# Order of the products at the seams of a two-layer encoder step: first product behind the fifth, earlier operand split, one set of PSUM pools, first scores inside the last projection

## The chip, the cores and the metric

The kernel runs on one core of a Trainium2 chip. The metric is the device time of one execution in microseconds (us). A core has five engines that run their own instruction queues in order: TensorE (PE, matrix products into PSUM; PEld is its weight load), VectorE (DVE), ScalarE (ACT), GpSimd (POOL) and SyncE (SP, which issues DMAs). An instruction waits at the head of its queue until all that it needs is there, and everything behind it on that engine waits too.

## The reference, cut to what matters

576 tokens (512 of a new stream, 64 of a running one) of width 1024 go through two layers. Layer 0 mixes tokens by pooling, layer 1 by sparse attention; each is followed by an MLP of width 4096.

```python
def _mlp(h, w_up, w_down):
    u = jax.nn.relu(h @ w_up)
    return (u * u) @ w_down

# attention, per query block: 8 index heads choose the keys, 16 heads attend to them
score = einsum('bth,bths->bts', wi, relu(qi . kidx * 64**-0.5)); _, idx = top_k(score, n_sel)
p = softmax(q . k[idx] * 64**-0.5);  o = p @ v[idx];  x = x + o @ w_o
```

New keys, values and index keys are outputs too.

## The kernel before, in words

**Numbers.** Every float32 operand is split into a high and a low part, and a product is three matmuls (high by high, high by low, low by high). Weights arrive as `raw`, ACT casts them to the high part `wh` (L182), DVE subtracts to the low part `wl` (L183); for some blocks POOL does the latter. Activations are split in `split_x` (`xs`: ACT L295, DVE L296).

**MLP.** A layer's MLP is done as 2 by 2 blocks with seven products in place of eight (`seven`, L526 to L554): first product b11, then t1 and t2, then b21, t3, b22 and t4. Three PSUM banks a, b and c collect them. "Up" is the first half with relu and square, "Down" the second. A product is 12 matmuls of 128x288 (`product`, L496 to L506, all recorded at L505). After the fifth product, t3, DVE's instruction L613 reads bank b; the last product, t4, goes on in the same bank, so it waits for L613. The first product b11 of the Down that follows belongs to another bank.

**Attention.** Its input is split to `xs` (eight tiles) and multiplied by the projection weights (`pj`); after the first two projections `norm.stats` sums squares (`st`, ten matmuls), a short chain on ACT and DVE turns them into the row scales, and `norm.spread` brings them to all partitions (`rb`). Index scores (`ix`, L1188 to L1216) are formed, for the fourth block (i = 4) by POOL with a multiply (L1213) and an add (L1215) for each of eight heads, and `top_k` (L1224) on DVE masks all but the chosen keys in 16 or 18 rounds of two instructions. Then 40 units (block i, key head g, half s) run as a pipeline in `steps`: `scores` (`sc`, softmax on DVE and ACT, division by the sum on POOL), `transpose` (`pt`, copied to `pT` by ACT), `values` (`o`), and for the blocks i below TURNED = 2 also `normalise` (`on`, DVE L1365) and in `outputs` a transpose (`ot`). The output projection is done in part ahead (`wa`) between the units, the rest (`wo`) at the end.

**What sets the order.** The code's order gives priorities, and a scheduler with a cost model orders each engine's queue when the program is built; the pools decide which buffer a tile lies on, and a tile waits until the buffer's last reader is done. Before the change the PSUM pools are opened anew for the attention (two tiles of two banks, four of one) and again for its units (three and two), and the `xs` of attention lie partly on buffers that the last Down still reads.

Of the kernel before, what the change touches and what calls it, by code (L numbers as in the profile page):

```python
# [1 line left out]

# [1 line left out]

# [6 lines left out]
F32R = mybir.dt.float32r  # L11
# [24 lines left out]
FINAL_ASIDE = ((4, 5), (4, 5))  # L36
NORM_STEPS = (4, 11, 13)
PACE = (1, 2, 2)
PACED = 3 * NIDX - 1
SLOTS = {"xs": 8, "a": 3, "b": 3, "c": 4, "d": 3, "e": 2}  # L40
TURNED = 2
AHEAD = 3
HEADS = {"a": 512, "c": 1024, "d": 1024}
UNITS = 6
UNDER = 64
SPREAD_AT = 5
SPARE_UNITS = 6
RAWS = (4, 3)
# [9 lines left out]
def pool_dsa_kernel(ctx: ExitStack, tc: tile.TileContext, a, o):  # L58
# [59 lines left out]
    def const(shape, name, dt=F32, pool=None):  # L118
        return (pool or cst).tile(shape, dt, tag=name, bufs=1, name=name)
# [278 lines left out]
    def mlp(layer, gi, late=0, end=None):  # L398
# [101 lines left out]
        def product(bank, w, operand, factor, js, first=False):  # L500
            for j in js:
                wh, wl = (t[:, j * P:(j + 1) * P] for t in w)
                uh, ul = (operand(j, factor, part) for part in range(2))
                for i, (wt, ut) in enumerate(((wh, uh), (wh, ul), (wl, uh))):
                    pe.matmul(bank[:, :HT], wt, ut, start=first and j == 0 and i == 0, stop=j == 3 and i == 2,  # L505
                              skip_group_check=True)  # L506

        tasks = [0]

        def ahead(n=1):  # L510

# [7 lines left out]
        def take():  # L519
            if not ready:  # L520
                ahead()
            return ready.pop(0)

        def seven(operand, late, on):


            b, a_, c = (psum1(t) for t in "bac")
            on.banks = [t[:, :HT] for t in (a_, b, c)]
            w = take()
            product(b, w, operand, "b11", rows, True)  # L530
            tasks[0] += 1
            if tasks[0] <= SEEDED:
                pe.matmul(a_[:, :HT], w[0][:, :P], operand(0, "b11", 0), start=True, stop=True, skip_group_check=True)
            act.copy(a_[:, :HT], b[:, :HT])  # L534
            ahead()
            w1 = take()
            if late:
                w2 = take()
                product(c, w1, operand, "t1", rows[:3], True)
                product(b, w2, operand, "t2", rows[:3])  # L540
                product(c, w1, operand, "t1", rows[3:])
                on.c()
                ahead()
                product(b, w2, operand, "t2", rows[3:])
            else:
                product(c, w1, operand, "t1", rows, True)
                on.c()
                ahead()
                product(b, take(), operand, "t2", rows)
            on.b()  # L550
            ahead()
            for bank, factor, then in ((a_, "b21", on.lo0), (b, "t3", on.hi1), (c, "b22", on.hi0), (b, "t4", on.lo1)):
                product(bank, take(), operand, factor, rows)
                then()  # L554

        class Down:


            def __init__(self, q):
                self.lo, self.hi = ([x[2 * q + i][:, c0:c0 + HT] for i in range(2)] for c0 in (HT, 0))  # L560
# [481 lines left out]
            nc.sync.dma_start(o["pool"][s], tail[:, s])  # L1042


    def attention(parts):
        nonlocal x
        norm = Norm("a")
        twos = []
# [11 lines left out]
        for j in range(KT // 2):  # L1060
            nc.sync.dma_start(xd[:, 2 * j:2 * j + 2], x.t[j])
        cst = phase["cst2"]
        cs, sn = const([P, T], "cs", pool=phase["under"]), const([P, T], "sn", pool=cst)
        nc.sync.dma_start(cs, a["cos"])
        nc.sync.dma_start(sn, a["sin"])
        V = const([P, 9, 256], "V", pool=cst)
# [78 lines left out]

        pki = psum1("ki"), psum1("ki")
        project(pki, next_block(), xs)
        qi = const([P, NIDX, T - P], "qi", F32R, phase["under"])
        between = iter(())
        rope_qi(0, started)  # L1150
        pt = psum1("pj"), psum1("pj")
# [31 lines left out]
        nc.sync.dma_start(o["v_p"], V[:, 0:4])  # L1183
        nc.sync.dma_start(o["v_s"], V[:TS, 8])

        work = [None] + [const([P, (i + 1) * P if i < 4 else TP + TS], f"work{i}", pool=cst) for i in range(1, 5)]

        def index_scores(i):  # L1188
            np_ = P if i < 4 else TS
            wk = work[i]  # L1190
            n = wk.shape[1]
            q = qi[:, :, (i - 1) * P:(i - 1) * P + np_]
            on_pool = i == 4
            for h in range(NIDX):
                if i < 4:
                    pf = psum1("ix")
                    for part in range(2):
                        pe.matmul(pf[:, :n], q[:, h], kis[:, part, :n], start=part == 0, stop=part == 1)
                else:
                    pf = psum("ix")  # L1200
                    for part in range(2):
                        for c in range(2):
                            pe.matmul(pf[:TS, c, :HT], q[:, h], cki[:, part, c * HT:(c + 1) * HT], start=part == 0, stop=part == 1)
                if i < 4:
                    rl = pf
                    act.activation(rl[:, :n], pf[:, :n], AF.Relu, scale=0.125)
                else:
                    rl = tmp("rl")
                    act.activation(halves(rl[:TS]), pf[:TS, :, :HT], AF.Relu, scale=0.125)
                wcol = wi[:np_, i, h:h + 1]  # L1210
                if on_pool:
                    dst = rl[:np_, :n] if h else wk[:np_]
                    pool.tensor_tensor(dst, rl[:np_, :n], wcol.to_broadcast([np_, n]), ALU.mult)  # L1213
                    if h:
                        pool.tensor_tensor(wk[:np_], wk[:np_], dst, ALU.add)  # L1215
                elif h == 0:  # L1216
                    dve.tensor_scalar(wk[:np_], rl[:np_, :n], wcol, None, ALU.mult)
                else:
                    dve.scalar_tensor_tensor(wk[:np_], rl[:np_, :n], wcol, wk[:np_], ALU.mult, ALU.add)
                yield  # L1220
            if i < 4:
                dve.memset(wk[0:64, i * P + 64:(i + 1) * P], NEG)
# [10 lines left out]
                dve.tensor_scalar(wk[64:128], wk[0:64], -2e38, NEG, ALU.is_gt, ALU.mult)  # L1233
            dve.tensor_scalar(wk[:np_], wk[:np_], -2e38, NEG, ALU.is_gt, ALU.mult)

        mask0 = const([P, P], "mask0", pool=cst)
        pool.memset(mask0, 0.0)
        pool.memset(mask0[0:64, 64:128], NEG)
        work[0] = mask0
# [19 lines left out]
        class Unit:  # L1259
# [5 lines left out]
            def scores(self):  # L1265
# [2 lines left out]
                q = self.group.q  # L1268
                mask = work[i]
                pr = slot("c", "p", F32)  # L1270
                pt = psum("sc")
                if i < 4:
                    n = (i + 1) * P
                    nw = max(n, 256)
# [128 lines left out]
        def steps():  # L1403

            ranked = {0}
            for u in range(-AHEAD - 2, total + 2):
                if 0 <= u + AHEAD + 2 < total and units[u + AHEAD + 2].s == 0:
                    v = units[u + AHEAD + 2]
                    groups[v.i, v.g] = Group(v.i, v.g)
                if 0 <= u < total:  # L1410
                    units[u].transpose()
                if 0 <= u + AHEAD < total:
                    v = units[u + AHEAD]
                    if u + AHEAD >= 4:
                        next(index, None)
                    if v.i not in ranked:
                        ranked.add(v.i)
                        while done[0] < v.i * NIDX and next(index, 1) is None:
                            pass
                        top_k(v.i)  # L1420
                    v.scores()
                if 0 <= u - 1 < total:
                    units[u - 1].values()
                if 0 <= u - 2 < total and units[u - 2].s == 1:
                    units[u - 2].group.outputs()
                if u >= 18 and u % 2 == 0:
                    next(first_out, None)
                yield

        def pace():  # L1430

            due = 0
            for k in range(10 * KT):
                while due <= k and done[0] < PACED:
                    next(index)
                    due += PACE[min(done[0] // NIDX, 2)]
                    done[0] += 1
                yield

        done = [0]  # L1440
        index = (None for i in range(1, 5) for _ in index_scores(i))
        act.activation(small(8, "e1", 1), wi[:, 0], AF.Exp)
        between = pace()
        qd, ks = {}, []
        (k1, k2), st = rope(False)
# [6 lines left out]
            ks.append(t)  # L1452
        for g in range(NKV):
            qd[g] = rope_q(f"q{g}", g == NKV - 2, pool.tensor_copy if g == NKV - 1 else act.copy)
        parts.close()
        parts.enter_context(stage(ps=3, po=2))
        for _ in steps():
            pass
        act.activation(small(2, "rt2", 1), units[-1].group.sums, AF.Sqrt)
        for _ in first_out:  # L1460
# [5 lines left out]
        for m in range(KT):  # L1466
            pool.tensor_tensor(x[m][:, :2 * P], x[m][:, :2 * P], ahead[m], ALU.add)
        for m in range(KT):
            pt = psum("wo")
            project(pt, next_block(), ot, cols=((2 * P, T - 2 * P),))  # L1470
            dve.tensor_tensor(x[m][:, 2 * P:], x[m][:, 2 * P:], pt[:, 0, :T - 2 * P], ALU.add)

    x = Residual()
    with stage(more=RAWS[1]):
        with stage(xs=1, slots=1, tmps=6, ps=3, po=2):
            pool_mixer()
        with stage(xs=1, u=1, acts=1, xt=1, sums=4, ps=2, po=4):
            mlp(0, 1, late=KT)
    with stage(under=1, xs=1, slots=1, cst2=1, tmps=5), ExitStack() as parts:
        const([P, UNDER], "pad", pool=phase["under"])  # L1480
        parts.enter_context(stage(ps=2, po=4))
        attention(parts)
    with stage(u=1, xs=1, acts=1, xt=1, sums=4, more=RAWS[1], ps=2, po=4):
        mlp(1, 3, end=last)


# [94 lines left out]
```

## Time and profile before

| what | value |
|---|---|
| median of 3 runs | 1087.51 us (1086.35 to 1089.1) |
| the profiled execution | 1087.99 us |
| its span on the core | 1086.2 us |
| PE, DVE, ACT, POOL busy | 97%, 84%, 58%, 24% |

The profile gives, for one execution, when each instruction began and how long it took; in brackets behind a row stands how long its engine had been idle before it and which instruction ended that. Matmuls overlap: rows of 128x288 begin 0.13 us apart though each is shown with some 0.3 us. In a table by windows PEclk is the clock that TensorE was granted, as a share of its full 2.4 GHz; half of it is 1.2 GHz. The timeline puts the span in stages: pooling and the MLP of layer 0 to 418 us, attention's projections from there to 541 us, its units to 662 us, the output projection to 692 us, the MLP of layer 1 to the end.

### The profile page before, as it was taken

What the parts mean: (1) busy time and instruction counts of PE and PEld (TensorE: products, weight loads), DVE (VectorE), ACT (ScalarE), POOL (GpSimd) and SP (SyncE); (2) the same over time, 40 slices, a digit from 0 to 9 for tenths busy, and PEclk for the clock granted to TensorE, in tenths of its full rate; (3) what the DMA queues carried; (4) which work ended last, traced back from release to release, by engine and by line L of the source; (5) the groups of instructions that cost most, each with busy time, mean ns of one, the idle gap of its engine ahead of it and who ended that gap; (6) DMA issues with size and microseconds to landing.
All of it is one profiled execution on the core that took longest, in us unless ns stands there. A gap on an engine that the chain in (4) does not pass through costs nothing.

```text
span 1086.2 us, 21647 instructions
## 1 busy us (share of the span) xinstructions
PE 1050.9 (97%) x7942; PEld 1023.6 (94%) x7942; DVE 909.0 (84%) x1845; ACT 629.3 (58%) x1240; POOL 263.8 (24%) x285
## 2 busy tenths in 40 slices
PE   8999999999999999999989999999999999999996
PEld 8999998999999998999978888999999999999895
DVE  7888989879978977879998944688989879979974
ACT  8555466447546645454378786555467447547641
POOL 3100111111111100217687893000111111111001
PEclk9999999999999999999999999999999999999998
DMA  8333665666666664456642454433666666666512
GB/s 251 92 101 90 173 165 151 166 163 168 150 167 163 156 171 144 123 167 175 201 114 59 133 158 140 136 108 96 167 160 161 161 169 162 155 169 161 123 51 88
DMA packets 94459, 157.66 MB, mean 145 GB/s; under 512 B 13729, under 2 KB 25296, under 8 KB 94352
## 3 DMA queue, kind: packets, MB, share of 16 engines
q1 hardware_dynamic: 68720, 109.80, 31.9%
q0 software_dynamic: 15840, 28.84, 16.8%
q10 hardware_dynamic: 9792, 17.63, 5.1%
q8 instruction: 62, 1.02, 0.4%
q14 instruction: 45, 0.37, 0.1%
HBM read 141.15 MB, written 10.89 MB: 140 GB/s over the span
## 4 chain that ended last, share of the span: by engine, by line
PE 75%; DVE 12%; DMA 4%; ACT 3%; issue 3%; POOL 2%; SPq 0%; ACTq 0%; DVEq 0%; POOLq 0%
PE b L505 28%; PE c L505 14%; PE up L306 9%; PE a L505 7%; PE pj L306 3%; DVE wl L183 3%; PE wo L306 3%; DVE work L1231 2%; PE sc L1278 2%; DVE m L1230 2%; PE wa L306 1%; PE pt L1304 1%; PE pb L1012 1%; PE dn L306 1%; DVE u L477 1%
## 5 line engine op out<-in xcount | busy, mean ns | idle before, releaser
L182 ACT CAST wh<-raw 128x512 fp32r<-128x512 f32 (+1 forms) x316 | 195.1, 620 | 233.3 <-PE b L505 75.7
L183 DVE TENSOR_TENSOR wl<-raw,wh 128x512 fp32r<-128x512 f32 (+1 forms) x294 | 206.6, 705 | 35.6 <-ACT wh L182 28.1
L505 PE MATMUL b<-u,wh 128*128 128x288 f32 x992 | 203.2, 296 | 3.4 <-ACT a L534 1.6
L505 PEld LDWEIGHTS b<-u,wh 128*128 128x128 f32 x992 | 159.7, 188 | 5.5 <-ACT a L534 3.6
L182 ACT CAST wh<-sum 128x512 fp32r<-128x512 f32 x165 | 101.4, 620 | 82.9 <-PE b L505 37.5
L505 PE MATMUL b<-u,wl 128*128 128x288 f32 x496 | 145.7, 296 | 0.0
L183 DVE TENSOR_TENSOR wl<-sum,wh 128x512 fp32r<-128x512 f32 x165 | 112.0, 687 | 23.3 <-ACT wh L182 21.2
L239 POOL DMA_DIRECT2D sum<-in_w_down x31 | 27.1, 893 | 327.6 <-DMA sum<-in_w_down 128.7
L505 PE MATMUL c<-u,wh 128*128 128x288 f32 x496 | 103.3, 297 | 0.8 <-DVE u L477 0.5
L505 PEld LDWEIGHTS b<-u,wl 128*128 128x128 f32 x496 | 92.7, 188 | 0.0
L306 PE MATMUL up<-xs,wh 128*128 128x288 f32 x512 | 89.5, 296 | 0.2
L505 PE MATMUL b<-xt,wh 128*128 128x288 f32 x384 | 78.1, 297 | 8.0 <-DVE v L613 8.0
L477 DVE TENSOR_TENSOR u<-v,u 128x864 fp32r<-128x864 f32 (+2 forms) x100 | 82.0, 824 | 0.9 <-ACT u L474 0.5
L505 PEld LDWEIGHTS c<-u,wh 128*128 128x128 f32 x496 | 80.1, 188 | 2.3 <-DVE x L563 1.5
L474 ACT CAST u<-v 128x864 fp32r<-128x864 f32 (+2 forms) x100 | 72.7, 730 | 8.3 <-DVE v L492 5.6
L505 PE MATMUL b<-xs,wh 128*128 128x288 f32 x384 | 76.9, 295 | 0.0
L306 PEld LDWEIGHTS up<-xs,wh 128*128 128x128 f32 x512 | 74.6, 188 | 1.0 <-DVE v L463 0.6
L505 PE MATMUL c<-u,wl 128*128 128x288 f32 x248 | 73.3, 296 | 0.0
L239 POOL DMA_DIRECT2D sum<-in_w_up x24 | 20.8, 865 | 210.1 <-DVE wl L183 114.3
L505 PEld LDWEIGHTS b<-xt,wh 128*128 128x128 f32 x384 | 61.4, 188 | 9.6 <-DVE v L613 9.6
L306 PE MATMUL pj<-xs,wh 128*128 128x288 f32 x352 | 61.9, 295 | 1.3 <-ACT xs L295 1.2
L455 ACT ACTIVATE v<-v 128x288 f32<-128x288 f32 (+1 forms) x112 | 52.1, 476 | 17.2 <-DVE v L596 14.7
(287 smaller groups left out, 2731.3 us busy)
## 6 DMA issues: line engine op xcount, KB each, us to landing
raw<-in_w_up SPq DMA_DIRECT2D x128, 256.0 KB, 3.0
raw<-in_w_down SPq DMA_DIRECT2D x128, 256.0 KB, 2.8
raw<-in_w_o ACTq DMA_DIRECT2D x32, 256.0 KB, 3.0
sum<-in_w_down SPq DMA_DIRECT2D x31, 256.0 KB, 2.6
sum<-in_w_down POOLq DMA_DIRECT2D x31, 256.0 KB, 4.4
raw<-in_w_down POOLq DMA_DIRECT2D x31, 256.0 KB, 5.0
raw<-in_w_in ACTq DMA_DIRECT2D x30, 256.0 KB, 3.3
sum<-in_w_up SPq DMA_DIRECT2D x24, 256.0 KB, 2.8
```

The lines of the kernel that those rows point to most:

```text
L182: act.copy(h, src)
L183: how["sub"].tensor_tensor(l, src, f32(h), ALU.subtract)
L239: pool.dma_start(s1, odd[:, 512:], accum_op=ALU.add)
L306: pe.matmul(pt[h][:, :m] if isinstance(pt, tuple) else pt[:, h, :m], wt, xs[k][:, part, c:c + m], start=(k == 0 and i == 0), stop=(k == n ...
L455: act.activation(v, v, AF.Square)
L474: act.copy(u[:, f, 0], v[:, f])
L477: dve.tensor_tensor(u[:, f, 1], v[:, f], f32(u[:, f, 0]), ALU.subtract)
L505: pe.matmul(bank[:, :HT], wt, ut, start=first and j == 0 and i == 0, stop=j == 3 and i == 2, skip_group_check=True)
L1012: pe.matmul(pt[:, c0:c0 + rhs.shape[1]], lhs, rhs, start=n == 0, stop=n == len(steps) - 1)
L1230: dve.max(m8[:np_], wk[:np_])
L1231: dve.match_replace(wk[:np_], m8[:np_], wk[:np_], TAKEN)
L1278: pe.matmul(pt[:, hh, :nw], q[:, 2 * s + hh], ks[g][:, part, :nw], start=part == 0, stop=part == 1)
```

## The change

Six edits go together.

- In `seven`, when a Down follows the final Up, its first product is issued behind t3's last matmul (`tc.issue_after`).
- One set of PSUM pools (two tiles of two banks, four of one) serves from the MLP of layer 0 to that of layer 1. The scores of units with i below 2 and the output projection take one-bank tiles.
- The SBUF pools are laid out so that the attention's `xs` lie where the MLP's own `xs` lay; `qi` has a pool of its own behind them, `cs`, `sn`, one work tile and a mask take the place of the weight buffers.
- Five steps of the unit pipeline run inside the last projection (FIRST_STEPS), and all 24 index heads of blocks 1 to 3 are paced inside the projections.
- For block i = 4, the multiply by `wi` goes from POOL to ACT.
- For i below 2, `outputs` comes one unit later.

```diff
-PACED = 3 * NIDX - 1
+PACED = 3 * NIDX
+FIRST_STEPS = (66, 68, 70, 73, 76)
...
-            product(b, w, operand, "b11", rows, True)
+            with tc.issue_after(behind.pop()) if late and behind else nullcontext():
+                product(b, w, operand, "b11", rows, True)
...
-                product(bank, take(), operand, factor, rows)
+                ins = product(bank, take(), operand, factor, rows)
+                if factor == "t3" and on.final:
+                    behind.append(ins.ins)
...
-        cs, sn = const([P, T], "cs", pool=phase["under"]), const([P, T], "sn", pool=cst)
+        cs, sn = (const([P, T], s, pool=phase["under"]) for s in ("cs", "sn"))
...
-        qi = const([P, NIDX, T - P], "qi", F32R, phase["under"])
+        qi = const([P, NIDX, T - P], "qi", F32R, phase["queries"])
...
-                    pool.tensor_tensor(dst, rl[:np_, :n], wcol.to_broadcast([np_, n]), ALU.mult)
+                    act.activation(dst, rl[:np_, :n], AF.Copy, scale=wcol)
...
-                pt = psum("sc")
+                if i < TURNED:
+                    pt = halves(psum1("sc"))
+                else:
+                    pt = psum("sc")
...
-                if 0 <= u - 2 < total and units[u - 2].s == 1:
-                    units[u - 2].group.outputs()
+                for v in units[max(u - 3, 0):max(u - 1, 0)]:
+                    if v.s == 1 and v is units[u - 3 if v.i < TURNED else u - 2]:
+                        v.group.outputs()
...
+                if k in FIRST_STEPS:
+                    next(unit_steps)
                 yield
...
-        parts.close()
-        parts.enter_context(stage(ps=3, po=2))
-        for _ in steps():
+        for _ in unit_steps:
...
-            pt = psum("wo")
-            project(pt, next_block(), ot, cols=((2 * P, T - 2 * P),))
-            dve.tensor_tensor(x[m][:, 2 * P:], x[m][:, 2 * P:], pt[:, 0, :T - 2 * P], ALU.add)
+            pt = psum1("wo")[:, :T - 2 * P]
+            project(pt.rearrange("p (o t) -> p o t", o=1), next_block(), ot, cols=((2 * P, T - 2 * P),))
+            dve.tensor_tensor(x[m][:, 2 * P:], x[m][:, 2 * P:], pt, ALU.add)
...
-    with stage(under=1, xs=1, slots=1, cst2=1, tmps=5), ExitStack() as parts:
-        const([P, UNDER], "pad", pool=phase["under"])
-        parts.enter_context(stage(ps=2, po=4))
-        attention(parts)
-    with stage(u=1, xs=1, acts=1, xt=1, sums=4, more=RAWS[1], ps=2, po=4):
+    with stage(under=1, xs=1, queries=1, slots=1, cst2=1, tmps=5):
+        attention()
+    with stage(u=1, xs=1, acts=1, xt=1, sums=4, more=RAWS[1]):
```

What it moves, at three places of PE's queue. Line numbers after the change are 7 to 13 higher. The first is the end of the layer-0 MLP, before: `b_5231<-u` is the last Down's t3 and then, with `wh_5281`, its t4; `pj` are the first matmuls of the attention's projections on the split input `xs`.

```order
L505 MATMUL b_5231<-u_4673,wh_5247 128x288 x2
L505 MATMUL b_5231<-u_4673,wl_5248 128x288
L505 MATMUL b_5231<-u_4208,wh_5281 128x288 x2
L505 MATMUL b_5231<-u_4208,wl_5282 128x288
L505 MATMUL b_5231<-u_4363,wh_5281 128x288 x2
L505 MATMUL b_5231<-u_4363,wl_5282 128x288
L505 MATMUL b_5231<-u_4518,wh_5281 128x288 x2
L505 MATMUL b_5231<-u_4518,wl_5282 128x288
L505 MATMUL b_5231<-u_4673,wh_5281 128x288 x2
L505 MATMUL b_5231<-u_4673,wl_5282 128x288
L306 MATMUL pj_5446<-xs_5392,wh_5298 128x288 x2
L306 MATMUL pj_5523<-xs_5392,wh_5336 128x288 x2
```

The same place after the change, from the last rows of t3 to the first of the projections:

```order
L505 MATMUL b_5231<-u_4673,wh_5247 128x288 x2
L505 MATMUL b_5231<-u_4673,wl_5248 128x288
L306 MATMUL pj_5440<-xs_5386,wh_5298 128x288 x4
L306 MATMUL pj_5517<-xs_5386,wh_5336 128x288 x4
L306 MATMUL pj_5440<-xs_5386,wl_5299 128x288 x2
L306 MATMUL pj_5440<-xs_5386,wh_5298 128x288 x4
L306 MATMUL pj_5440<-xs_5386,wl_5299 128x288 x2
L306 MATMUL pj_5440<-xs_5395,wh_5298 128x288 x4
L306 MATMUL pj_5440<-xs_5395,wl_5299 128x288 x2
L306 MATMUL pj_5440<-xs_5395,wh_5298 128x288 x4
L306 MATMUL pj_5440<-xs_5395,wl_5299 128x288 x2
L306 MATMUL pj_5440<-xs_5406,wh_5317 128x288 x4
```

Forty projection matmuls in all now stand between t3 and t4 (six more follow the rows shown), where none stood.

A little later on PE stand the sums of squares `st` and the spreading of the scales `rb`, before:

```order
L356 MATMUL st_5503<-ones,s_875_5391 64x96
L306 MATMUL pj_5523<-xs_5401,wh_5336 128x288
L306 MATMUL pj_5523<-xs_5401,wl_5337 128x288 x2
L306 MATMUL pj_5523<-xs_5412,wh_5355 128x288 x4
L306 MATMUL pj_5523<-xs_5412,wl_5356 128x288 x2
L306 MATMUL pj_5523<-xs_5412,wh_5355 128x288 x4
L306 MATMUL pj_5523<-xs_5412,wl_5356 128x288 x2
L306 MATMUL pj_5523<-xs_5423,wh_5355 128x288 x4
L306 MATMUL pj_5523<-xs_5423,wl_5356 128x288 x2
L306 MATMUL pj_5523<-xs_5423,wh_5355 128x288 x4
L306 MATMUL pj_5523<-xs_5423,wl_5356 128x288 x2
L336 MATMUL rb_5588<-sq_5584,ones 128x288
```

And after the change:

```order
L356 MATMUL st_5497<-ones,s_874_5385 64x96
L306 MATMUL pj_5517<-xs_5417,wh_5355 128x288 x4
L306 MATMUL pj_5517<-xs_5417,wl_5356 128x288 x2
L306 MATMUL pj_5517<-xs_5417,wh_5355 128x288 x4
L306 MATMUL pj_5517<-xs_5417,wl_5356 128x288 x2
L336 MATMUL rb_5582<-sq_5578,ones 128x288
```

Between `st` and `rb` stood 27 matmuls, and 12 stand there now; 84 of the 96 that come before `rb` are ahead of `st`.

The third place is the start of the units, before: `pj_6820` is the last projection, `sc` are scores, `pt` transposes.

```order
L306 MATMUL pj_6820<-xs_5423,wh_6680 128x288 x4
L306 MATMUL pj_6820<-xs_5423,wl_6681 128x288 x2
L1278 MATMUL sc_6923<-k_6240,q_6917 128x256 x4
L1278 MATMUL sc_6935<-k_6240,q_6917 128x256 x4
L1278 MATMUL sc_6999<-k_6240,q_6920 128x256 x4
L1304 MATMUL pt_7010<-ident,p_6922 128x128 x2
L1278 MATMUL sc_7016<-k_6240,q_6920 128x256 x4
```

After the change, from the third of the scores on:

```order
L1288 MATMUL sc_6939<-k_6234,q_6811 128x256 x4
L306 MATMUL pj_6837<-xs_5406,wh_6679 128x288 x4
L306 MATMUL pj_6837<-xs_5406,wl_6680 128x288 x2
L306 MATMUL pj_6837<-xs_5406,wh_6679 128x288 x4
L306 MATMUL pj_6837<-xs_5406,wl_6680 128x288 x2
L306 MATMUL pj_6837<-xs_5417,wh_6679 128x288 x4
L306 MATMUL pj_6837<-xs_5417,wl_6680 128x288 x2
L306 MATMUL pj_6837<-xs_5417,wh_6679 128x288 x4
L306 MATMUL pj_6837<-xs_5417,wl_6680 128x288 x2
L1314 MATMUL pt_7001<-ident,p_6813 128x128 x2
L1288 MATMUL sc_7007<-k_6234,q_6811 128x256 x4
L1288 MATMUL sc_7036<-k_6239,q_6887 128x256 x4
```

The scores of the first three units lie among the projections, and the first transpose follows the last projection at once.

## Rows read from the trace of the kernel before

**Rows 1.** The page, busy time of each engine over the span.
```profile
PE 1050.9 (97%) x7942; PEld 1023.6 (94%) x7942; DVE 909.0 (84%) x1845; ACT 629.3 (58%) x1240; POOL 263.8 (24%) x285
```
**Rows 2.** PE's waits over the span: us in total, times, longest.
```profile
PE b L505 <- DVE v L613: 8.0, 7, 1.3
```
**Rows 3.** Busy us by window: PE, PEld, DVE, ACT, POOL, PEclk, DMA share, GB/s.
```profile
540.00:560.00 20.00, 16.89 (x123) 15.64 (x122) 18.47 (x72) 15.14 (x52) 18.02 (x16) 0.91 0.46 131
560.00:580.00 20.00, 16.92 (x127) 16.09 (x128) 16.45 (x62) 14.10 (x47) 14.80 (x12) 0.91 0.36 96
580.00:600.00 20.00, 19.68 (x172) 17.33 (x171) 19.30 (x58) 16.86 (x45) 16.15 (x25) 1.00 0.28 79
```
**Rows 4.** Timeline of PE, t3, b11 and t4: start, us, instruction, idle before.
```profile
184.89 0.29 PE L505 MATMUL b<-xs,wl 128*128 128x288 f32 x1
185.02 0.29 PE L505 MATMUL b<-u,wl 128*128 128x288 f32 x1
...
186.17 0.40 PE L505 MATMUL b<-u,wh 128*128 128x288 f32 x1
187.47 0.53 PE L505 MATMUL b<-xt,wh 128*128 128x288 f32 x2 [0.90 <-DVE v L613]
```
**Rows 5.** Timeline of DVE at the same place.
```profile
185.40 0.68 DVE L265 TENSOR_TENSOR sum<-sum,raw 128x512 f32<-128x512 f32 x1
...
186.97 0.45 DVE L613 TENSOR_TENSOR v<-b,snap 128x288 f32<-128x288 f32 x1
```
**Rows 6.** Timeline of PE, last Down to the scales.
```profile
412.95 0.43 PE L505 MATMUL b<-u,wh 128*128 128x288 f32 x2
...
414.40 0.29 PE L505 MATMUL b<-u,wl 128*128 128x288 f32 x1
416.07 0.50 PE L505 MATMUL b<-u,wh 128*128 128x288 f32 x2 [1.37 <-DVE x L563]
...
419.16 1.39 PE L306 MATMUL pj<-xs,wh 128*128 128x288 f32 x6 [1.25 <-ACT xs L295]
...
428.72 1.34 PE L356 MATMUL st<-ones,s 128*128 128x96 f32 x10
...
433.64 1.13 PE L336 MATMUL rb<-sq,ones 128*128 128x288 f32 x4
```
**Rows 7.** Timeline of DVE, the end of the scales' chain.
```profile
432.87 0.25 DVE L349 TENSOR_SCALAR sq<-ident,r 128x64 f32<-128x64 f32 x1
```
**Rows 8.** Timeline of PE, the first units.
```profile
542.08 1.68 PE L1278 MATMUL sc<-k,q 128*128 128x256 f32 x12 [1.34 <-ACT rp L1102]
544.81 0.71 PE L1304 MATMUL pt<-ident,p 128*128 128x128 f32 x2 [1.05 <-ACT p L1249]
...
570.57 0.44 PE L1374 MATMUL ot<-ident,on 128*128 128x128 f32 x2 [2.22 <-DVE on L1365]
```
**Rows 9.** Timeline of DVE, the first units.
```profile
550.57 0.42 DVE L1365 TENSOR_TENSOR on<-o,rs 128x256 f32<-128x256 f32 x1 [1.15 <-PE o L1329]
...
572.30 0.29 DVE L1248 CUSTOM_DVE_ANT_0 p<-sc,mask 128x128 f32<-128x128 f32 x1 [1.38 <-PE sc L1278]
...
576.03 0.42 DVE L1248 CUSTOM_DVE_ANT_0 p<-sc,work 128x256 f32<-128x256 f32 x1 [1.25 <-PE sc L1278]
```
**Rows 10.** Groups by line and shape, 540 to 640 us: busy us, mean ns, idle before.
```profile
L1209 ACT ACTIVATE rl<-ix 64x576 f32<-64x576 f32 x8 | 5.1, 638 | 0.1
...
L1248 DVE CUSTOM_DVE_ANT_0 p<-sc,work 128x512 f32<-128x512 f32 x16 | 10.4, 685 | 4.0 <-PE sc L1278 3.9
...
L1248 DVE CUSTOM_DVE_ANT_0 p<-sc,work 128x384 f32<-128x384 f32 x16 | 8.2, 550 | 0.6 <-PE sc L1278 0.5
```
**Rows 11.** The same view, POOL, 540 to 662 us.
```profile
L1213 POOL TENSOR_TENSOR rl<-rl,wi 64x576 f32<-64x576 f32 x7 | 8.0, 1143 | 4.9 <-ACT rl L1209 4.9
L1467 POOL TENSOR_TENSOR x<-x,wo 128x256 f32<-128x256 f32 x8 | 5.7, 737 | 1.8 <-DMA x<-xd 1.6 <-DVE nm L1248 0.2
```
**Rows 12.** Timeline of PE, start of the output projection.
```profile
662.08 0.54 PE L306 MATMUL wo<-ot,wh 128*128 128x320 f32 x2
```

More of the change, by code (lines that the diff above doesn't have):

```diff
@@ L1 @@
-from contextlib import ExitStack, contextmanager
+from contextlib import ExitStack, contextmanager, nullcontext
 import numpy as np
@@ L44 @@
 UNITS = 6
-UNDER = 64
 SPREAD_AT = 5
@@ L504, in product @@
                 for i, (wt, ut) in enumerate(((wh, uh), (wh, ul), (wl, uh))):
-                    pe.matmul(bank[:, :HT], wt, ut, start=first and j == 0 and i == 0, stop=j == 3 and i == 2,
-                              skip_group_check=True)
+                    ins = pe.matmul(bank[:, :HT], wt, ut, start=first and j == 0 and i == 0, stop=j == 3 and i == 2,
+                                    skip_group_check=True)
+            return ins
         tasks = [0]
+        behind = []
         def ahead(n=1):
@@ L552, in seven @@
             for bank, factor, then in ((a_, "b21", on.lo0), (b, "t3", on.hi1), (c, "b22", on.hi0), (b, "t4", on.lo1)):
-                product(bank, take(), operand, factor, rows)
+                ins = product(bank, take(), operand, factor, rows)
+                if factor == "t3" and on.final:
+                    behind.append(ins.ins)
                 then()
         class Down:
+            final = False
             def __init__(self, q):
@@ L1042, in pool_mixer, with attention @@
             nc.sync.dma_start(o["pool"][s], tail[:, s])
-    def attention(parts):
+    def attention():
         nonlocal x
@@ L1184, in attention @@
         nc.sync.dma_start(o["v_s"], V[:TS, 8])
-        work = [None] + [const([P, (i + 1) * P if i < 4 else TP + TS], f"work{i}", pool=cst) for i in range(1, 5)]
+        work = [None] + [const([P, (i + 1) * P if i < 4 else TP + TS], f"work{i}", pool=phase["under"] if i == 1 else cst) for i in range(1, 5)]
         def index_scores(i):
@@ L1234, in top_k @@
             dve.tensor_scalar(wk[:np_], wk[:np_], -2e38, NEG, ALU.is_gt, ALU.mult)
-        mask0 = const([P, P], "mask0", pool=cst)
+        mask0 = const([P, P], "mask0", pool=phase["under"])
         pool.memset(mask0, 0.0)
@@ L1442, in attention @@
         act.activation(small(8, "e1", 1), wi[:, 0], AF.Exp)
+        unit_steps = steps()
         between = pace()
@@ L1468, in attention @@
         for m in range(KT):
-            pt = psum("wo")
-            project(pt, next_block(), ot, cols=((2 * P, T - 2 * P),))
-            dve.tensor_tensor(x[m][:, 2 * P:], x[m][:, 2 * P:], pt[:, 0, :T - 2 * P], ALU.add)
+            pt = psum1("wo")[:, :T - 2 * P]
+            project(pt.rearrange("p (o t) -> p o t", o=1), next_block(), ot, cols=((2 * P, T - 2 * P),))
+            dve.tensor_tensor(x[m][:, 2 * P:], x[m][:, 2 * P:], pt, ALU.add)
     x = Residual()
+    psums = ctx.enter_context(ExitStack())
     with stage(more=RAWS[1]):
@@ L1476, in pool_dsa_kernel @@
             pool_mixer()
-        with stage(xs=1, u=1, acts=1, xt=1, sums=4, ps=2, po=4):
+        banks = psums.enter_context(ExitStack())
+        banks.enter_context(stage(ps=2, po=4))
+        with stage(xs=1, u=1, acts=1, xt=1, sums=4):
             mlp(0, 1, late=KT)
-    with stage(under=1, xs=1, slots=1, cst2=1, tmps=5), ExitStack() as parts:
-        const([P, UNDER], "pad", pool=phase["under"])
-        parts.enter_context(stage(ps=2, po=4))
-        attention(parts)
-    with stage(u=1, xs=1, acts=1, xt=1, sums=4, more=RAWS[1], ps=2, po=4):
+    with stage(under=1, xs=1, queries=1, slots=1, cst2=1, tmps=5):
+        attention()
+    with stage(u=1, xs=1, acts=1, xt=1, sums=4, more=RAWS[1]):
         mlp(1, 3, end=last)
```

## The prediction, made before the changed kernel was run

> **What bounds the kernel now.** I read the engines' busy times first, to see who is short of time: PE is at 97% [rows 1], so only some 35 us of the span can be won on PE without taking work from it, and none of the six edits takes a matmul away. So the question is where PE stands idle, and who holds it there. The list of PE's waits gives the largest: 8.0 us in seven pieces for DVE's L613, at the seam of each final Up and its Down [rows 2]. The windows then show the one stretch where PE is clearly short of work: 540 to 580 us, where it is busy 16.89 and 16.92 of 20 us and has a mean granted clock of 0.91, and 1.00 in the window behind [rows 3]. From 580 us it is full again, 19.68 of 20. The timelines show what each wait stands behind.
>
> **First product behind t3.** It moves one product of PE's queue past another in each of seven seams and adds no work. A matmul of this size takes 0.132 us from start to start (the first and the twelfth of a product at 412.95 and 414.40 [rows 6]), so up to 12 of them would give 1.6 us of cover to the wait before t4. The trace has a seam that already looks almost as it will after the change: in the one at 187 us, t3's last matmul starts at 184.89, then eight matmuls of the Down's first product run, from 185.02 to 186.17, and still t4 waits 0.90 us for L613 [rows 4]. L613 doesn't wait for t3 there: it stands in DVE's queue as the last of four instructions that run without a gap from 185.40 on [rows 5], a sum, a weight subtraction and an L596 ahead of it. More cover on PE does not make DVE come to L613 sooner, so I take 0 for the edit. The bounds: at best all 8.0 us go [rows 2]; at worst a seam that had no wait gets the mean one, 8.0 / 7 = 1.1 us.
>
> **Earlier split.** At 412.95 us the last Down's t3 starts, and its last matmul makes way at 414.5; then PE waits 1.37 for DVE's x and 1.25 for the first `xs`, and `st` starts at 428.72 and `rb` at 433.64 [rows 6]. In the new order 40 projection matmuls fill the first wait, and the split tiles that they read no longer lie on buffers that this Down holds. I work it forward: 414.5 + 40 x 0.132 = 419.8; t4 takes 1.6, to 421.4; 44 more take 5.8, to 427.2; `st` takes the 1.34 of its row, to 428.6. What is late next is the scales' chain: the last matmul of `st` ended at 430.06, its successor on DVE at 432.87 + 0.25 = 433.12 [rows 6, 7], 3.1 us. So `rb` can't start before 428.6 + 3.1 = 431.7, and the 12 matmuls that now stand between cover only 1.6 of it: of the 2.6 us of waits, some 0.7 are left over, since a wait of 1.5 comes up at `rb` where 27 matmuls covered the chain before; the index key's projection stands behind it on PE, the multiplies by the cosines and sines on POOL and DVE. The gain is 433.64 - 431.7 = 1.9 us. The eight splits are hidden by DVE's and ACT's idle time in the Down; without that cover each would cost up to the wait that its first reader had, 1.25. On SP the load of the sines goes behind those that save x; it is needed only after `rb`, so 0. Bounds: 2.6 at best; 0 at worst, if the x updates behind the splits on DVE come late by as much.
>
> **Scores in the last projection, outputs later, one set of pools.** Before, the first scores wait 1.34 for the projection's banks to be emptied (rp) since the pools are opened anew, and the first transpose waits 1.05 for the first softmax; later PE waits 2.22 for `on`, with scores queued behind that `ot` [rows 8]. All three lose their reason: the scores lie among projection matmuls, their softmax runs meanwhile, and `ot` comes a unit later. That is 4.6 us of PE. But the stretch is not PE's alone. DVE is busy 18.47 of 20 us there with top_k, then 16.45 [rows 3], and the moved softmaxes lengthen its queue ahead of 540 us by as much as they shorten it behind. DVE can end earlier only by its own idle time, and of that the trace shows 1.15 (for `o`), 1.38 and 1.25 (for `sc`, both behind the `ot` that waited) [rows 9], 3.8 together. I take 3.0: the two waits for `sc`, 2.6, in full, and a third of the first. Bounds: 0, if top_k alone sets the pace, and the idle time of PE in the two windows, 3.11 + 3.08 = 6.2, plus what the half clock takes there, 0.09 x 40 = 3.6.
>
> **The multiply on ACT.** Eight POOL multiplies of 1.14 us go, 9.1 us [rows 11], and eight ACT instructions of the same 64x576 come. The trace has no such copy; the nearest rows are the relu of the same shape, 0.64 us [rows 10], as the lower end, and POOL's 1.14 itself as the upper: 5.1 to 9.1 us on an ACT that idles 4.9 + 5.9 us in the two windows [rows 3]. I take 5.1, hidden. So POOL and ACT roughly trade places, and the fourth block's top_k can start a few units sooner. What it brings PE is within the 3.0 above, since PE is full from 580 us.
>
> **Behind 580 us** PE idles 0.3 us of 20 [rows 3], so it keeps what it has won, if nothing new holds it. POOL's additions of the first half of x wait 1.6 us for a load of x [rows 11] and now stand slightly earlier in POOL's queue; cover is the output projection behind them, so 0.
>
> **Sum.** 0 - 1.9 - 3.0 = -4.9 us against the profiled execution's 1087.99, its span of 1086.2 and 1.8 around it: 1083.1. That execution is 0.5 above the median of the runs; against the median it is 1082.6.
>
> **Rivals.**
>
> - *DVE sets the pace of the first units.* Speaks for it: 18.47 of 20 busy. Against: 3.8 us of idle time that is due to PE. Then only the split's 1.9 is left: 1087.5 - 1.9 = 1085.6.
> - *The split's gain does not come* (the splits are made in time, but the chain to `rb` holds all). For it: the cover of that chain falls from 27 to 12 matmuls. Then 1087.5 - 3.0 = 1084.5.
> - *PE takes all it can.* The clock is at its upper level throughout, and PE's idle time of 540 to 580 us goes, 6.2 + 3.6, with the split's 1.9: 11.7 less, 1075.8 at the end of it; with two thirds of the 11.7, which I take for it, 1079.7. Against: DVE. A part of the seams' 8.0 us would lead to the same place.
> - *Slower: two tiles of two banks where there were three.* The 24 units of the blocks from i = 2 on put scores and transposes in turn on these. With two tiles, the next unit's scores take the tile that the last unit's softmax still reads on DVE; with three there was one to spare. Price: PE would stand for the second half of the softmax, 0.685 or 0.55 us [rows 10], mean 0.62, in each of the 16 units of i = 2 and 3, 9.9 us in all, since PE is full there. It decides as soon as PE finds no `wa` matmul ahead of the scores to do meanwhile. 1087.5 + 9.9 - 4.9 = 1092.5. Against: between 580 us and the start of `wo` [rows 12] the 24 units take 82 / 24 = 3.4 us each, and the two halves of a softmax at most 1.4 of that [rows 10], so the tile is as a rule free in time. The Trainium skill, "Perfetto Trace Analysis", section Matmuls, wants independent matmul groups to rotate over PSUM banks, so that the emptying of one overlaps the next. The Trainium skill's same page, section Optimization Strategy, reads gaps that repeat on an engine that should be full as a possible sign of too little PSUM. By that skill's rule fewer pairs lengthen the time as in this rival; the trace of before, with PE at 19.68 of 20 [rows 3], shows three pairs to be enough and does not show two.
>
> **How the numbers follow.** Chances: forecast 0.44, DVE 0.22, no split gain 0.08, PE takes all 0.15, slower 0.11. The likeliest case's own range, from its bounds, is 1080 to 1086. A measurement of this kernel tells 0.3%, 3.3 us, from no change: that is 1084.2 and 1090.8. The forecast lies 1.6 us beyond the first bound and would hold beyond it in four cases of five: 0.44 x 0.82 + 0.15 = 0.51 faster. Slower: 0.11. The rest, 0.38, is no change. The range leaves out the best part of "PE takes all" and most of the slower rival: 1076.5 to 1089.5.
>
> **What would show it.** Right: `pj` between t3 and t4 without a wait for x and `xs`, and a wait of about 1.5 us at `rb`, which starts near 431.7; the first `pt` some 4 us earlier, near 540.5 (the projections end at 542.08 - 1.34 = 540.74, less 1.9, and the 1.68 of the scores among them [rows 8]), with no wait for rp or p; no 2.2 us wait at `ot`; t4's seven waits for L613 about as long in sum as before; the start of `wo`, 662.1 before [rows 12], near 657; from there the same distance to the end. Wrong: waits of `sc` or `pt` that repeat for 0.3 us or more in the units from i = 2; a gain at t4 of several us (then L613 was waiting for t3, not for DVE); a start of `wo` that has not moved, which would mean that POOL's chain, not PE, sets the units' pace.

## The result and the profile after

The changed kernel takes 1095.01 us (1093.91 to 1095.53), the kernel before 1087.47 in the same comparison: 1.0069 times as long, 95% interval 1.0057 to 1.0081. I had forecast 1082.6; it is 7.5 us slower, the side of the rival that I gave 0.11.

The profiled execution of the changed kernel has a span of 1093.8 us, 7.6 more than before. Its page shows the same engines at nearly the same busy time [rows 1]:

```profile
PE 1054.4 (96%) x7942; PEld 1024.6 (94%) x7942; DVE 910.2 (83%) x1845; ACT 633.1 (58%) x1248; POOL 254.0 (23%) x277
```

PE is busy 3.5 us longer with the same work and idle 4.1 us longer; the windows say where. The columns are those of [rows 3]:

```profile
540.00:560.00 20.00, 16.53 (x130) 15.09 (x129) 19.83 (x75) 17.91 (x56) 18.56 (x15) 1.00 0.51 147
560.00:580.00 20.00, 16.03 (x119) 14.52 (x117) 19.79 (x66) 15.18 (x47) 6.43 (x6) 0.95 0.36 95
580.00:600.00 20.00, 19.67 (x149) 17.83 (x148) 16.77 (x46) 12.73 (x32) 12.90 (x19) 0.88 0.21 57
600.00:620.00 20.00, 19.51 (x169) 16.46 (x169) 18.89 (x47) 14.16 (x33) 16.04 (x21) 1.00 0.42 132
...
660.00:680.00 20.00, 18.38 (x157) 15.64 (x156) 7.17 (x17) 12.54 (x29) 7.63 (x12) 1.00 0.35 94
```

Two things differ from before. From 540 to 580 us DVE, the third of the counted columns, is full: 19.83 and 19.79 of 20, where it had been 18.47 and 16.45, while PE idles longer. And from 580 us on PE is no longer quite full, and has a clock of 0.88 in the first window, 0.12 x 20 = 2.4 us short of the full one.

The timeline of PE gives the places of [rows 6, 8, 12]; the row at 542.01 is the first transpose, those of 128x384 and 128x512 are the first scores of i = 2 and of i = 3, and the last is the start of the output projection:

```profile
426.97 1.33 PE L356 MATMUL st<-ones,s 128*128 128x96 f32 x10
...
431.86 1.24 PE L336 MATMUL rb<-sq,ones 128*128 128x288 f32 x4 [1.77 <-DVE sq L346]
...
542.01 0.38 PE L1314 MATMUL pt<-ident,p 128*128 128x128 f32 x2
...
573.60 0.94 PE L1288 MATMUL sc<-k,q 128*128 128x384 f32 x4
...
606.90 1.09 PE L1288 MATMUL sc<-k,q 128*128 128x512 f32 x4
...
670.62 0.56 PE L306 MATMUL wo<-ot,wh 128*128 128x320 f32 x2
```

`rb` is 1.8 us earlier than before and the first transpose 2.8, but the output projection begins 8.5 us later. All that is lost is lost in the units, and most of it in the eight of i = 2: from their first scores to the first scores of i = 3 it is 33.3 us now, 4.2 a unit, and it was 24.2, 3.0 a unit:

```profile
576.81 0.95 PE L1278 MATMUL sc<-k,q 128*128 128x384 f32 x4
...
600.99 1.09 PE L1278 MATMUL sc<-k,q 128*128 128x512 f32 x4
```

PE's waits over the whole span after the change, us in total, times, longest:

```profile
PE b L505 <- DVE v L620: 8.1, 8, 1.3
PE rb L336 <- DVE sq L346: 1.8, 1, 1.8
PE sc L1288 <- ACT pT L1315: 1.7, 1, 1.7
...
PE pt L1314 <- ACT pT L1315: 1.6, 3, 1.0
PE pt L1314 <- ACT rl L1216: 1.3, 1, 1.3
PE pt L1319 <- POOL ck L293: 1.0, 1, 1.0
...
PE pt L1314 <- ACT rp L1109: 1.0, 1, 1.0
...
PE ix L1205 <- DVE wi L1189: 0.8, 1, 0.8
...
PE pj L306 <- DVE rp L1105: 0.7, 1, 0.7
```

The seams' wait, 8.0 before [rows 2], stays at 8.1 (L620 is the old L613). The waits for p, x and xs are gone, and the one for `on` fell from 2.2 to 0.5 us. For rp PE waited 1.3 before, at the first scores; now it waits 1.0 at a transpose and 0.7 in the projections. In place of the waits that went, scores and transposes wait for `pT`, ACT's copy of a transpose out of its two-bank tile, 3.3 us in all.

### The profile page after: what moved, and what is told of

It is laid out like the page before. It is cut to its first block, busy times and chain, and to the rows that moved or that the text cites. A ratio compares the mean times of both kernels' runs of the same rounds, so it can differ in the third digit from the quotient of the medians.

```text
span 1093.8 us, 21614 instructions
## 1 busy us (share of the span) xinstructions
PE 1054.4 (96%) x7942; PEld 1024.6 (94%) x7942; DVE 910.2 (83%) x1845; ACT 633.1 (58%) x1248; POOL 254.0 (23%) x277
## 4 chain that ended last, share of the span: by engine, by line
PE 77%; DVE 9%; ACT 4%; DMA 3%; POOL 3%; issue 3%; SPq 0%; ACTq 0%; DVEq 0%; POOLq 0%
PE b L505 29%; PE c L505 15%; PE up L306 9%; PE a L505 7%; PE pj L306 5%; PE wo L306 3%; DVE wl L183 1%; PE wa L306 1%; PE pb L1019 1%; DVE work L1238 1%; PE dn L306 1%; PE pt L1314 1%; DVE m L1237 1%; DVE u L477 1%; ACT wh L182 1%
## 5 line engine op out<-in xcount | busy, mean ns | idle before, releaser
L505 PEld LDWEIGHTS b<-u,wl 128*128 128x128 f32 x496 | 92.7, 188 | 0.0
```

The lines of the kernel that those rows point to most:

```text
L505: ins = pe.matmul(bank[:, :HT], wt, ut, start=first and j == 0 and i == 0, stop=j == 3 and i == 2, skip_group_check=True)
```

## The experiments

Theory A: the multiply on ACT brings the fourth block's top_k early and into the way. Theory B: the PSUM pools and the early scores. Theory C: the later outputs. Ratios are against runs of the kernel before on the same chip.

**e1_poolmul**: the multiply back on POOL.
```diff
-act.activation(dst, rl[:np_, :n], AF.Copy, scale=wcol)
+pool.tensor_tensor(dst, rl[:np_, :n], wcol.to_broadcast([np_, n]), ALU.mult)
```


> The changed kernel with the multiply by wi for block 4 back on POOL; all else as changed. Theory A (the multiply on ACT makes the fourth block's scores complete earlier, so that its top_k rounds stand among the softmaxes of the first units on DVE, and ACT, which copies pT, is fuller): 1095 falls to 1090 or below, the first round of top_k for 64 rows starts near 578 in place of 569.6. Theory B (two PSUM tiles of two banks where there were three hold the units back): no change, 1094 to 1096. Theory C (outputs one unit later): no change.

Measured: 1100.5 us, ratio 1.0120 (1.0103 to 1.0138), slower still, where theory A wanted 1090 or below. This run alone does not refute it, since PE has a new wait that could hide a gain; e2 and e3, which have the multiply on ACT and lose nothing, do. The new wait:

```profile
PE sc L1288 <- DMA q<-q: 7.3, 1, 7.3
```

The scores of the last key head wait for their q, which POOL splits (`st`) behind the multiplies. POOL's timeline:

```profile
560.68 2.25 POOL L1220 TENSOR_TENSOR rl<-rl,wi 64x576 f32<-64x576 f32 x2
562.89 1.42 POOL L1120 TENSOR_TENSOR st<-rp,st 128x576 fp32r<-128x576 f32 x1
...
566.73 1.42 POOL L1120 TENSOR_TENSOR st<-rp,st 128x576 fp32r<-128x576 f32 x1
```

**e2_ps3**: the pools opened anew for the units, no scores in the projection.
```diff
+        banks.close()
+        banks.enter_context(stage(ps=3, po=2))
         for _ in unit_steps:
...
-FIRST_STEPS = (66, 68, 70, 73, 76)
+FIRST_STEPS = ()
```
(scores of all units and the output projection on two-bank tiles again, PACED = 23, and the pools set back behind the attention)

> The changed kernel with the PSUM pools opened anew for the units as before the change (three tiles of two banks, two of one), so that no scores run in the last projection; the earlier split, the multiply on ACT, the later outputs and the product order stay as changed. Theory B: 1095 falls to 1085.5 to 1088. Theory A: it stays at 1092 or above, since the rounds of top_k still come early. Theory C: it stays near 1095.

Measured: 1085.3 us, ratio 0.9975 (0.9965 to 0.9984): faster than both kernels, 9.7 us below the changed one. Theory B holds. Its windows:

```profile
540.00:560.00 20.00, 17.41 (x114) 15.93 (x112) 17.67 (x69) 15.87 (x52) 15.27 (x13) 0.83 0.38 115
560.00:580.00 20.00, 18.11 (x146) 17.11 (x146) 19.26 (x72) 19.55 (x61) 8.99 (x9) 1.00 0.41 107
580.00:600.00 20.00, 19.93 (x176) 17.36 (x177) 19.15 (x53) 15.77 (x41) 17.20 (x26) 1.00 0.24 69
600.00:620.00 20.00, 20.00 (x181) 16.95 (x177) 18.32 (x46) 15.42 (x34) 16.76 (x21) 1.00 0.51 156
```

PE is full again from 580 us, and DVE has room before.

**e3_before_actmul**: the kernel before with the multiply on ACT (the edit of e1 the other way round).

> The kernel before with one edit, the multiply by wi on ACT. Theory A: 1087.5 rises to 1091 or more. Theories B and C: 1086 to 1088.5.

Measured: 1085.9 us, ratio 0.9989 (0.9980 to 0.9999). A small gain, some 1.2 us, where theory A wanted 1091 or more.

**e4_outputs_early**: outputs of i below 2 two units behind, as before.
```diff
-                for v in units[max(u - 3, 0):max(u - 1, 0)]:
-                    if v.s == 1 and v is units[u - 3 if v.i < TURNED else u - 2]:
-                        v.group.outputs()
+                if 0 <= u - 2 < total and units[u - 2].s == 1:
+                    units[u - 2].group.outputs()
```


> The changed kernel with outputs of the first blocks where they stood before, two units after the scores' unit in place of three. Theory C (they hold a one-bank tile of o longer, with the scores in the same four banks): 1095 falls to 1090 or below. Theories A and B: 1094 to 1098, since the wait for on comes back.

Measured: 1093.4 us, ratio 1.0053 (1.0034 to 1.0072). Theory C explains some 1.6 of the 7.5 us, inside the two intervals.

Theory B has two parts. The next four take them apart.

**e5_no_first**: no scores in the last projection (FIRST_STEPS = (), PACED = 23), pools as changed.

> The changed kernel without scores in the last projection (FIRST_STEPS empty); the one set of pools (two tiles of two banks, four of one) stays. Theory B1 (the units from i = 2 on lack the third tile of two banks): it stays slow, 1093 to 1097, and scores of units 16 to 23 still come some 4 us apart. Theory B2 (the scores drawn into the projection lengthen DVE's queue there and upset the order of what follows): 1085 to 1089.

Measured: 1091.4 us, ratio 1.0034 (1.0019 to 1.0049): 3.6 us better, 6.1 worse than e2.

**e6_first_ps3**: scores in the projection as changed, and the pools opened anew behind it (e2's first two added lines; the scores and the output projection behind them on two-bank tiles again).

> The changed kernel with the first five steps inside the last projection, as changed, and the pools opened anew behind it (three tiles of two banks, two of one) for all the other units and the output projection. Theory B1: 1085 to 1088, scores of units 16 to 23 some 2.7 us apart. Theory B2: 1092 or more.

Measured: 1090.9 us (1087.8 to 1092.5), ratio 1.0034 (1.0023 to 1.0045): 4.1 better, 5.6 worse than e2. Neither B1 nor B2 alone, and neither run falls into a range that I had given: the pools cost 4.1 to 6.1 us, the early scores 3.6 to 5.6, and together they are the 9.7.

**e7_ps3_early**: e2 with e4's edit.

> The changed kernel with the pools opened anew for the units (three and two), no scores in the projection, and outputs two units later as before the change: so the earlier split, the multiply on ACT and the first product behind t3 are all that is left. If the later outputs cost 1.6 us here too, as their removal gave in the changed kernel: 1083 to 1084.5 against 1085.3; if that cost belonged to the four one-bank tiles: no change. Against the kernel before with the multiply on ACT alone, 1085.9, the rest is what the split gives: my step says 1.9, or 0 if DVE takes it back at the index scores.

Measured: 1085.6 us, ratio 0.9980 (0.9970 to 0.9989). With three pairs the later outputs cost and bring nothing. Against e3 (0.9989) some 1 us is left for the split and the product order.

**e8_before_ps2**: the kernel before with one thing taken from the change.
```diff
-        parts.close()
-        parts.enter_context(stage(ps=3, po=2))
```


> The kernel before with one edit: the pools are not opened anew for the units, so that these have two tiles of two banks and four of one; all scores stay on two-bank tiles and behind the projection. Theory B1: 1087 rises to 1093 or more. Theory B2: 1086 to 1089.

Measured: 1095.3 us, ratio 1.0073 (1.0058 to 1.0088). Two pairs of banks, with four single ones beside them, alone slow the kernel before by 7.9 us. Of PE's waits from 540 to 675 us in this run, the three longest, and those of scores for a softmax (`nm`, what its DVE row writes):

```profile
PE sc L1278 <- ACT pT L1305: 1.8, 6, 0.4
PE pt L1304 <- POOL wl L183: 1.6, 1, 1.6
PE pt L1304 <- DVE nm L1248: 1.2, 1, 1.2
...
PE sc L1288 <- DVE nm L1248: 0.4, 1, 0.4
PE sc L1278 <- DVE nm L1248: 0.4, 2, 0.2
```

and of the kernel before, where one wait of scores for such a copy stood:

```profile
PE sc L1278 <- ACT pT L1305: 0.3, 1, 0.3
```

Scores now wait six times for a copy of `pT`, 1.8 us, and three times for a softmax, 0.8 us. I read it so: with two tiles the scores of a later unit lie on the tile of the last transpose. These waits are not the whole: all of PE's waits in this stretch sum to 8.8 us, and to 6.9 before, so most of the 7.9 us stands in no wait that the profile names. Rows of matmuls overlap, and short pauses between them may not show.

**e9_sc_one_bank**: the changed kernel, scores of i = 2 and 3 on two one-bank tiles, so that the pairs serve transposes (and the scores of i = 4).
```diff
+                elif i < 4:
+                    pair = psum1("sc"), psum1("sc")
```


> The changed kernel, but the scores of the units i = 2 and 3 take two one-bank tiles in place of one of the two two-bank tiles, so that these serve the transposes alone. If the third tile is missed because scores and transposes wait for each other's tile (scores for the copy pT on ACT): 1095 falls by 3 us or more, to 1092 or below. If four one-bank tiles for o, wa and scores are as short: 1095 or more.

Measured: 1091.5 us, ratio 1.0038 (1.0025 to 1.0051): 3.5 us better. The sharing of the pairs by scores and transposes is one cause.

**e10_ps3_no_behind**: e2 without `tc.issue_after`.

> As e2_ps3 (pools opened anew for the units), but the first product is not issued behind t3. My step says that this edit is worth 0, since DVE's queue, not t3, holds L613: 1084.5 to 1086, and t4's waits for L613 some 8 us in sum with it and without. If the edit was worth its cover of up to 1.2 us a seam: 1088 or more.

Measured: 1085.1 us, ratio 0.9978 (0.9968 to 0.9987). The edit is worth nothing, as forecast: PE waits 8.0 us in sum for DVE's read of bank b with it (e2) and without.

**e11_before_act_r12**: e3 with rounds of top_k left out.
```diff
-            for _ in range(16 if i < 4 else 18):
+            for _ in range((16, 16, 16, 12, 18)[i]):
```


> The kernel before with the multiply on ACT, and with 12 of the 16 rounds of top_k for block 3 (four rounds of 1.45 us are left out, so block 3 masks fewer keys). If DVE sets the pace from the index scores to the end of that top_k (480 to 570 us): 1085.9 falls by 3 us or more. If PE's own waits do: no change.

Measured: 1086.2 us, ratio 0.9990 (0.9981 to 1.0000). Nothing: DVE does not set that kernel's pace, although it is nearly full in this window of e3 (third counted column):

```profile
540.00:560.00 20.00, 16.80 (x129) 14.94 (x128) 19.48 (x73) 17.11 (x56) 16.48 (x14) 1.00 0.51 142
```

**e12_split_act_r12**: e7 with the same edit.

> As e7_ps3_early (earlier split, first product behind t3, multiply on ACT, pools as before), and with the same four rounds of top_k for block 3 left out. If the split's 1.9 us were lost to DVE, which is full from 480 to 570 us, they show again here: 1.5 to 2 us below e11_before_act_r12. If they are lost elsewhere: within 0.5 us of it.

Measured: 1085.5 us, ratio 0.9983 (0.9974 to 0.9993), within the interval of e11. The split's 1.9 us do not come back, so they were not lost to these rounds.

It was still open how the early scores cost time.

**e13_first_ps3_r12**: e6 with e11's edit.

> As e6_first_ps3 (scores in the last projection, pools opened anew behind it), with four of the 16 rounds of top_k for block 3 left out, so that block 3 masks fewer keys. In the kernel before these rounds were worth nothing. If the early scores cost time since DVE, not PE, then sets the pace: 1090.9 falls by 3 us or more, to 1088 or below. If not: 1090 to 1092.

Measured: 1087.6 us, ratio 1.0002 (0.9992 to 1.0011): 3.3 us better. With the scores in the projection DVE's work counts. Windows of e6:

```profile
540.00:560.00 20.00, 15.87 (x127) 14.62 (x127) 19.73 (x69) 17.46 (x50) 18.92 (x15) 1.00 0.51 147
560.00:580.00 20.00, 15.64 (x123) 14.39 (x123) 19.57 (x71) 16.84 (x55) 6.88 (x6) 1.00 0.37 99
```

and of e13, where DVE has 4.4 us less to do in the second, and PE 1.4 us less to wait:

```profile
560.00:580.00 20.00, 17.04 (x133) 15.25 (x131) 15.20 (x61) 17.63 (x56) 7.87 (x8) 1.00 0.38 102
```

Part of the 3.3 us may be clock: TensorE's mean granted clock over all executions is 0.9947 in e6 and 0.9967 here, by my estimate at most 0.002 x 1090 = 2.2 us. The two profiled executions, whose windows above all have the full clock, differ by 0.9 us in span (1087.2 and 1086.3).

**e14_r12**: the changed kernel with e11's edit.

> The changed kernel with the same four rounds left out. If DVE sets its pace between 536 and 580 us: 1095 falls by 3 us or more. If the tiles do (PE waiting for copies of pT and for softmaxes, one after the other): less than 1.5 us.

Measured: 1090.4 us, ratio 1.0025 (1.0014 to 1.0037): 4.6 us better, where the same edit gave nothing in e11. DVE's work counts in the changed kernel too. Here as well part may be clock, 0.9938 in the changed kernel and 0.9962 in this one: at most 0.0024 x 1093 = 2.6 us by the same estimate.

**e15_sc_one_bank_no_first**: e9 and e5 together.

> The changed kernel with scores of i = 2 and 3 on two one-bank tiles (as e9) and without scores in the last projection (as e5). If the shared pairs and the early scores are the two causes and add up, 3.5 and 3.6 us: 1087 to 1088.5. If four one-bank tiles for scores, o, wa and ot are a third: 1089.5 or more.

Measured: 1087.8 us, ratio 1.0001 (0.9993 to 1.0010). Taking away the shared pairs (but for i = 4) and the early scores takes away the loss against the kernel before. Against e2 some 2.8 us are left (1.0001 and 0.9975), and what they belong to is not shown.

Nor is the loss gone from the units. From the first scores of i = 2 to the first matmul of the output projection the profiled executions take 85.3 us before, 85.8 in e2 and 86.7 in e6, which have three pairs there; with two pairs they take 97.0 (changed), 94.6 (e5), 93.0 (e9), 92.7 (e15) and 89.8 (e8). In the changed kernel, e5, e9 and e15 between 1 and 2 us of that are `values` matmuls that stand elsewhere in the others. What e15 loses there it gains by starting i = 2 sooner, at 570.4 us, against 576.8 before and 574.1 in e2.

## Why the prediction was wrong

**The step that failed is the third, "Scores in the last projection, outputs later, one set of pools": forecast -3.0 us, measured +9.7 (changed kernel against e2; e2 keeps the later outputs, which e7 finds to be worth nothing there).** Three things in it:

- *The pools.* I had the mechanism as a rival, with one releaser of several and too little weight. I priced the wait as half a softmax, 0.62 us for 16 units, and argued against it with 3.4 us a unit. That was a mean over all 24. The timeline of DVE before the change has the softmaxes of the first units of i = 2 only 2.3 us apart, (584.59 - 577.81) / 3, where, as I read it, the scores run ahead on the third tile (first lines below this list); and I counted the softmax but not the transposes and the copy to `pT` that hold the other tile. Measured: 7.9 us (e8), 4.1 (changed against e6), 6.1 (e5 against e2), 3.5 by one-bank scores (e9). By the Trainium skill, "Perfetto Trace Analysis", section Matmuls, groups should rotate over PSUM banks so that emptying overlaps the next product; e8 agrees: one pair fewer cost 7.9 us.
- *The early scores.* I called their softmaxes neutral for DVE, as much ahead as less behind. Measured, early scores cost 3.6 us with two pairs (e5) and 5.6 with three (e6 against e2). With them DVE has no room left (19.83 and 19.79 of 20 us): without them four rounds of top_k less are worth nothing (e11), with them 3.3 to 4.6 us (e13, e14), clock included. Which instruction they push back is open. It is not the end of top_k for i = 3: its last instruction starts at 568.5 us, and at 569.8 before. And e5 does not take the early scores away alone: the scheduler orders DVE's queue anew, and there that instruction starts at 583.2 (second lines below: before, changed, e5).
- *DVE's idle time as a gain.* The 3.8 us that I counted did go, and PE's three waits went, from 4.6 us to 1.5. PE then waited elsewhere for the same DVE, by way of ACT (third lines below, changed kernel): scores that are done at 573.4 get their softmax on the full DVE at 576.05; ACT waits 1.63 for it; the copy to `pT` stands behind that in ACT's queue; and the next scores wait 1.66 for the copy.

```profile
577.81 0.56 DVE L1248 CUSTOM_DVE_ANT_0 p<-sc,work 128x384 f32<-128x384 f32 x1
...
579.56 0.56 DVE L1248 CUSTOM_DVE_ANT_0 p<-sc,work 128x384 f32<-128x384 f32 x1
...
581.91 0.54 DVE L1248 CUSTOM_DVE_ANT_0 p<-sc,work 128x384 f32<-128x384 f32 x1
...
584.59 0.54 DVE L1248 CUSTOM_DVE_ANT_0 p<-sc,work 128x384 f32<-128x384 f32 x1
```

```profile
569.75 0.43 DVE L1234 TENSOR_SCALAR work<-work 128x512 f32<-128x512 f32 x1
...
568.48 0.78 DVE L1241 TENSOR_SCALAR work<-work 128x512 f32<-128x512 f32 x1
...
583.23 0.62 DVE L1241 TENSOR_SCALAR work<-work 128x512 f32<-128x512 f32 x1
```

```profile
572.68 0.72 PE L1288 MATMUL sc<-k,q 128*128 128x256 f32 x4
...
576.05 0.41 DVE L1255 CUSTOM_DVE_ANT_0 p<-sc,work 128x256 f32<-128x256 f32 x1
...
576.50 0.51 ACT L1256 ACTIVATE p<-p,nm 128x256 f32<-128x256 f32 x1 [1.63 <-DVE nm L1255]
...
577.75 0.58 ACT L1315 COPY pT<-pt 128x512 f32<-128x512 f32 x1
...
578.38 1.65 PE L1288 MATMUL sc<-k,q 128*128 128x384 f32 x4 [1.66 <-ACT pT L1315]
```

**The second step, the split, -1.9 us: right at its place, not at the end.** `rb` came at 431.86, forecast 431.7, with a wait of 1.77, forecast 1.5. (Of the forty matmuls ahead of t4, eight and not six follow the rows shown for that place.) On the way to the units 1.5 us went to two new waits on DVE, for wi and for rp, between 440 and 540 us, and the first transpose came at 542.0 in place of 540.5. e7 against e3 leaves some 1 us, inside the two intervals. Where the rest goes in e7 stays open: e12 says that it is not top_k's rounds.

**The first step, 0 for the product order: right.** L613 is waited for 8.1 us as before, and e10 measures nothing.

**The multiply on ACT, counted within the 3.0: worth 1.2 us by itself in the kernel before** (e3, interval 0.1 to 2.2 by its ratio), and more in the changed one, where POOL has the last q to split as well (e1, 5.5 us).

**The rivals.** "DVE sets the pace of the first units" I took for a smaller gain. It does not hold in the kernel before, as far as four rounds tell (e11, with the multiply on ACT), and becomes a loss after. "Slower: two tiles" ended at 1092.5, close to the 1095.0. The closeness is in part luck: its 9.9 us for the pools measured 4.1 to 7.9, and the 4.9 us of gains that it took off did not come. Its direction deserved more than 0.11: the change took a resource away in a stretch where PE was full, and I had no row that showed the smaller amount to be enough.

## What to carry to other kernels

Moving work earlier on an engine that is idle puts its followers earlier on an engine that may be full; look at the queue of the second engine, and time the kernel with some of that engine's work left out. A busy share of 19.5 of 20 us does not tell whether an engine sets the pace: four rounds taken from DVE were worth nothing in e11 and 4.6 us, clock included, in e14. And when buffers are merged or shared, price them where the units come fastest, with every holder of the buffer in the loop, not by the mean.

## What the runs showed of the hardware

In most of the profiled executions TensorE's granted clock falls to its lower level, 1.2 GHz, for a few us at the start of attention or in its units, but not at the same place; in e3, e6, e11, e13 and e15 it does so only behind the last matmuls. In the changed kernel it fell behind PE's idle time at 576 us (windows of 4 us, columns as above):

```profile
576.00:580.00 4.00, 2.34 (x13) 2.20 (x11) 4.00 (x16) 3.12 (x10) 0.31 (x1) 0.76 0.01 3
580.00:584.00 4.00, 4.00 (x20) 3.90 (x19) 2.65 (x8) 1.42 (x5) 1.58 (x3) 0.50 0.23 66
584.00:588.00 4.00, 3.67 (x27) 3.21 (x27) 3.94 (x12) 2.75 (x8) 2.19 (x4) 0.89 0.01 4
```

Here it hits the stretch in which PE is otherwise full, while before [rows 3] and in e2 (0.83 from 540 to 560 us) it lay ahead of 580 us, where PE had to wait anyway. And it differs from execution to execution of the same kernel: e6 took 1089.0 us at a mean clock of 0.998 and 1092.5 at 0.993. So one profile of a kernel tells its time to some 3 us only, and the differences above are taken from medians. Medians do not take the clock out, since kernels differ in it too: the mean over all executions was 0.9943 in the kernel before and 0.9966 in e15, the same time with some 0.0023 x 1087 = 2.5 us (an estimate) less of clock lost.
